# A two-stage encoder trunk on one core: its engine queues put in order by the context's timeline model instead of its default one

## The chip, the cores and the metric

The kernel runs on one core of one Trainium2 chip. A core has a matrix engine (TensorE, PE in the profile), a vector engine (DVE), a scalar engine (ACT), GpSimd (POOL) and a queue that issues transfers (SyncE, SP). Each engine works down one queue of instructions in the order in which the program lists them. The metric is the device time of one execution in microseconds (us), lower is better. Before the change the median of three runs was 2829.97 us, the lowest 2828.54 and the highest 2830.24.

## The reference, cut to what matters

A stream of 2048 frames with 1024 channels passes two layers.

- Layer 0: RMS norm, one projection to `u` and `z`; `u` goes through trailing means over 2, 4, 8 and 16 frames minus the frame itself, a linear map per channel group and a scale; times SiLU(z), an output projection, and a residual add. Then a gated embedding: `x + (p[0] @ ple_w[0]) * sigmoid(x @ ple_gate_w[0])`.
- From the stream after layer 0 one projection gives keys (RMS-normed) and values for 16 heads of 64 channels.
- Layer 1: RMS norm, a projection to `q` and `z`, RMS norm of `q` per head, strictly causal stick-breaking attention, times SiLU(z), output projection, residual add, and a second gated embedding.

The attention is what the second stage spends its time on:

```python
mask = s_idx < t_idx
log_keep = jnp.where(mask, jax.nn.log_sigmoid(-logits), 0.0)
later = lax.cumsum(log_keep, axis=log_keep.ndim - 1, reverse=True) - log_keep
log_a = jax.nn.log_sigmoid(logits) + later
a = jnp.where(mask, jnp.exp(log_a), 0.0)
```

So a weight is sigmoid(logit) times the product of (1 - sigmoid) over all later keys that are still visible. All inputs are float32, the output is float32 of 2048 x 1024.

## The kernel before, in words

Every float32 operand of a product is split into a high and a low part, and each product is three matmuls (high x high, high x low, low x high). The frames are cut into four chunks of 512.

**Stage one** runs layer 0, the key and value projection and the query projection, chunk by chunk, 22 steps for each chunk (`run_u`, `run_z`, `run_m`, `run_o`, `run_g`, `run_kvq`). A step is a product of 48 to 96 matmuls into a PSUM pool of six buffers (`psd`), and the vector, scalar and GpSimd engines empty it. Keys, queries, values and the split weights of stage two go to DRAM.

**Stage two** runs the attention. The loop goes over query chunks `c` = 3, 2, 1, 0, in each over 16 heads, and in each over the key chunks from the diagonal one backwards. One (query chunk, head, key chunk) is a slot of four sub-steps. Each sub-step has three parts, at three different sub-steps of the loop:

- `front`: two matmuls give 128 queries x 512 keys of logits (lines L602 and L603, tile `psl`, two buffers). ACT makes sigmoid(-logit) from it (L606, tile `kap`, four buffers). On the diagonal POOL masks a piece of it (L608). DVE scans it with a running product (L613, tile `pp`, 12 buffers).
- `turn`, six sub-steps later: PE transposes four 128 x 128 pieces of `pp` (L627) into a tile `psa`. ACT copies that to the high part of `at` (L630), DVE subtracts to get the low part (L631). `psa` has two buffers, so the transposes of a turn wait until L631 of the turn two earlier has read its buffer.
- `gather`, two sub-steps after the turn: PE multiplies the values with the high part (L639) and the low part (L640) into `pso`.

There are 160 slots and so 640 turns: 256 for c = 3, 192 for c = 2, 128 for c = 1, 64 for c = 0.

Beside the attention a generator of other matmuls, called fillers here (L668, L670, L672, 512 columns each), is pulled at a fixed rate: in c = 3 the gate projection `z` of the four chunks (`gate_z`), three matmuls per sub-step; in c = 2, 1 and 0 the output projection and the gated embedding of the chunk that was finished before (`post`). After the last slot `post(0)` runs alone.

```python
for n in range(4 * len(slots) + LAG_G):
    i2, j2 = divmod(n - LAG_T, 4)
    if 0 <= i2 < len(slots):
        turn(active[i2], j2)
    ...
        scan = front(active[i], j)
    if scan is not None:
        scan()
    owed += rate
    while owed >= 1.0:
        next(filler, None)
        owed -= 1.0
    ...
        gather(active[i3], j3)
```

**What sets the order.** The code above gives each instruction its place in a program, and that place is its priority. When the context closes, a scheduler plays the program through a model of the machine, and each time an engine is free it takes from the instructions that the model holds for ready the one with the earliest place. The order in which the model took them is then fixed as the engine's queue. A few instructions of stage one are tied to their place (`tc.keep_in_program_order`). On the chip nothing is rearranged any more: an instruction at the head of a queue that has to wait holds all those behind it.

## Time and profile before

| | |
|---|---|
| median of three runs | 2829.97 us (2828.54 to 2830.24) |
| profiled execution, first to last instruction (span) | 2822.5 us; no device time of its own is listed for it, 7.5 us less than the median |
| PE busy | 2747.1 us, 97% |
| DVE busy | 1892.6 us, 67% |
| ACT busy | 1409.9 us, 50% |
| POOL busy | 953.8 us, 34% |
| mean granted TensorE clock | 0.996 |

Stage one takes the first 1395 us of the span; the first turn of stage two starts at 1415.4 and the last at 2712.7 us; the rest is `post(0)`. PE is busy in nine tenths or more of all slices but two. DVE is half busy in stage one and nearly always busy in the first two thirds of stage two: 282.39 of the 300 us from 1600 on, 290.87 of the 300 us from 1900 on. A "busy" time of two neighbours on DVE overlaps a little, so the shares are a bit high.

### The profile page before, as it was taken

The numbers are of one execution on the slowest core, as the hardware profiler recorded it, in microseconds if no ns is written. First come the engines' busy times: TensorE is split into PE (matmuls) and PEld (weight loads), VectorE is DVE, ScalarE is ACT, GpSimd is POOL, SyncE is SP. The second block draws the span as 40 slices with busy tenths as digits, with TensorE's granted clock in tenths as the row PEclk, the third lists the DMA queues.
The fourth block names the chain that finished last, engine by engine and source line by source line (L and its number), as shares of the span: only waits on it lengthen the run. The fifth ranks groups of instructions, "written<-read, shape, count | busy, mean of one in ns | idle before, by whom it ended". The sixth has DMA issues, their size and how long they took to land. (4 is left out here: it accounts for less than half of the span.)

```text
span 2822.5 us, 40373 instructions
## 1 busy us (share of the span) xinstructions
PE 2747.1 (97%) x13667; PEld 2271.8 (80%) x13667; DVE 1892.6 (67%) x2581; ACT 1409.9 (50%) x2765; POOL 953.8 (34%) x965
## 2 busy tenths in 40 slices
PE   8999999999999999999899999999999999999999
PEld 6788788888888888888778888887878778878877
DVE  6655534555355543445289999999999998886642
ACT  5445523455244542445356555666666665664431
POOL 3564346643475425644211112121211122223220
PEclk9999999999999999999999999999999999999999
DMA  7855695557855678446666565455555565658765
GB/s 270 274 173 205 238 317 166 175 208 246 303 167 176 221 248 285 147 147 203 213 198 218 185 208 177 161 168 183 171 162 171 168 189 183 195 184 262 242 203 160
DMA packets 335139, 576.43 MB, mean 204 GB/s; under 512 B 32782, under 2 KB 161838, under 8 KB 334932
## 3 DMA queue, kind: packets, MB, share of 16 engines
q1 hardware_dynamic: 327944, 564.34, 60.8%
q10 hardware_dynamic: 6988, 9.50, 1.1%
q8 instruction: 108, 1.77, 0.3%
q14 instruction: 99, 0.81, 0.1%
HBM read 433.16 MB, written 132.19 MB: 200 GB/s over the span
## 5 line engine op out<-in xcount | busy, mean ns | idle before, releaser
L356 PE MATMUL psd<-wpair,x 128*128 128x512 f32 x2304 | 544.0, 393 | 0.0
L630 ACT CAST at<-psa 128x512 fp32r<-128x512 f32 (+3 forms) x640 | 333.4, 522 | 404.8 <-PE psa L627 399.9
L613 DVE TENSOR_TENSOR_SCAN pp<-kap,pp,zeros 128x512 f32<-128x512 f32 x384 | 511.7, 1334 | 5.0 <-ACT kap L606 2.8
L356 PEld LDWEIGHTS psd<-wpair,x 128*128 128x128 f32 x2304 | 428.1, 188 | 86.3
L631 DVE TENSOR_TENSOR at<-psa,at 128x512 fp32r<-128x512 f32 (+3 forms) x640 | 379.7, 595 | 59.2 <-ACT at L630 56.5
L627 PE MATMUL psa<-ident,pp 128*128 128x128 f32 x2176 | 347.4, 275 | 25.0 <-DVE at L631 20.4
L606 ACT ACTIVATE kap<-psl 128x512 f32<-128x512 f32 (+3 forms) x640 | 343.9, 538 | 17.0 <-PE psl L603 8.2
L627 PEld LDWEIGHTS psa<-ident,pp 128*128 128x128 f32 x2176 | 263.3, 140 | 102.8 <-DVE at L631 45.7
L608 POOL TENSOR_SCALAR_AFFINE_SELECT kap<-kap 128x128 f32<-128x128 f32 x256 | 91.7, 359 | 626.8 <-ACT kap L606 532.3
L602 PE MATMUL psl<-kk,qa 128*128 128x512 f32 (+3 forms) x640 | 281.3, 440 | 4.2 <-ACT vr L393 3.5
L613 DVE TENSOR_TENSOR_SCAN pp<-kap,zeros 128x128 f32<-128x128 f32 (+3 forms) x256 | 213.9, 836 | 40.5 <-POOL kap L608 37.0
L640 PE MATMUL pso<-at,vv 128*128 128x512 f32 (+3 forms) x640 | 235.4, 368 | 0.0
L603 PE MATMUL psl<-kk,qb 128*128 128x512 f32 (+3 forms) x640 | 234.6, 367 | 0.0
L639 PE MATMUL pso<-at,vv 128*128 128x512 f32 (+3 forms) x640 | 232.5, 363 | 1.3 <-ACT at L630 1.2
L127 PE MATMUL psd<-xp,wpair 128*128 128x512 f32 x512 | 200.2, 391 | 2.4 <-ACT xp L172 2.4
L111 DVE SCALAR_TENSOR_TENSOR wpair<-wraw,gains,wpair 128x512 fp32r<-128x512 f32 x192 | 149.6, 790 | 78.4 <-ACT wpair L110 78.1
L128 PE MATMUL psd<-xp,wpair 128*128 128x512 f32 x512 | 200.1, 391 | 0.0
L129 PE MATMUL psd<-xp,wpair 128*128 128x512 f32 x512 | 199.8, 390 | 0.0
L110 ACT ACTIVATE wpair<-wraw,gains 128x512 fp32r<-128x512 f32 x192 | 136.8, 720 | 113.2 <-DMA wraw<-in_w_kv_dram 69.2
L106 POOL TENSOR_TENSOR wpair<-wraw,wpair 128x512 fp32r<-128x512 f32 x107 | 146.0, 1369 | 62.1 <-ACT wpair L104 40.7
L104 ACT CAST wpair<-wraw 128x512 fp32r<-128x512 f32 x160 | 97.7, 619 | 114.2 <-PE psd L129 109.1
L639 PEld LDWEIGHTS pso<-at,vv 128*128 128x128 f32 x640 | 120.5, 188 | 28.4 <-ACT at L630 2.6
(204 smaller groups left out, 5488.9 us busy)
## 6 DMA issues: line engine op xcount, KB each, us to landing
wpair<-wi SPq DMA_DIRECT2D x96, 512.0 KB
kk<-kd SPq DMA_DIRECT2D x320, 128.0 KB
vv<-vd SPq DMA_DIRECT2D x160, 256.0 KB
wraw<-in_w_kv_dram SPq DMA_DIRECT2D x128, 256.0 KB
wpair<-wzd SPq DMA_DIRECT2D x64, 512.0 KB
wpair<-wod SPq DMA_DIRECT2D x64, 512.0 KB
wpair<-wgd SPq DMA_DIRECT2D x64, 512.0 KB
wi<-wpair SPq DMA_DIRECT2D x32, 512.0 KB
```

The lines of the kernel that those rows point to most:

```text
L127: T.matmul(ps, wst(units, kt, 0, c0), acts[kt][:, 0], start=(kt == order[0]), stop=False)
L128: T.matmul(ps, wst(units, kt, 0, c0), acts[kt][:, 1], start=False, stop=False)
L356: T.matmul(pss2[i], ck["x2"][kt][:, xh, tk], wst(ws, kt, wh, 0, W5), start=(kt == 0 and xh == 0 and wh == 0), stop=(kt == KT - 1 and wh == 1))
L602: T.matmul(ps[:, :w], qa[:, qs], kk[:, :w], start=True, stop=False)
L603: T.matmul(ps[:, :w], qb[:, qs], kk[:, :w], start=False, stop=True)
L606: A.activation(out=kp[:, r0:], in_=ps[:, :w], func=AF.Sigmoid, scale=-1.0)
L613: V.tensor_tensor_scan(out=pp[:, r0:][:, ::-1], data0=kp[:, r0:][:, ::-1], data1=zeros.to_broadcast([P, w]), initial=1.0 if st["diag"] els ...
L627: T.transpose(pt[:, j * P : (j + 1) * P], pp[:, r0 + kt * P : r0 + (kt + 1) * P], ident)
L630: A.copy(out=at[:, 0, cs], in_=pt[:, cs])
L631: V.tensor_tensor(out=at[:, 1, cs], in0=pt[:, cs], in1=f(at[:, 0, cs]), op=ALU.subtract)
L639: T.matmul(po[:, cs], vv[:, kt, :], at[:, 0, cs], start=(st["diag"] and kt == 0), stop=False)
L640: T.matmul(po[:, cs], vv[:, kt, :], at[:, 1, cs], start=False, stop=(st["last"] and kt == 3))
```

## The change

One argument of the context: the scheduler plays the program through the timeline model instead of the default one. The program, its priorities, its buffers and the number of arithmetic instructions stay the same.

```diff
-    with _tile.TileContext(nc) as tc:
+    with _tile.TileContext(nc, schedule_with_timeline_sim=True) as tc:
         trunk_kernel(tc, *args)
```

All five queues come out in another order. In stage one the matmuls of a product stay nearly where they were: no matmul of a product moves by more than about 9 us of PE work. In stage two the change is large. Instructions that only wait for a semaphore go from 411 to 572 on PE and from 719 to 1168 on DVE.

First place: PE, while the gate projection of an earlier chunk runs beside the attention of query chunk 3 (`xz` is that chunk's input, `psd` the fillers' result). Before:

```order
L627 MATMUL psa<-ident,pp 128x128 x4
L602 MATMUL psl<-kk,qa 128x512
L603 MATMUL psl<-kk,qb 128x512
L668 MATMUL psd<-xz,wpair 128x512
L670 MATMUL psd<-xz,wpair 128x512
L672 MATMUL psd<-xz,wpair 128x512
L639 MATMUL pso<-at,vv 128x512
L640 MATMUL pso<-at,vv 128x512
```

Each turn had its logits, three fillers and one gather. In the changed kernel the queue has this just ahead of the second such projection:

```order
L627 MATMUL psa<-ident,pp 128x128 x4
L640 MATMUL pso<-at,vv 128x512
L639 MATMUL pso<-at,vv 128x512
L627 MATMUL psa<-ident,pp 128x128 x4
L640 MATMUL pso<-at,vv 128x512
L639 MATMUL pso<-at,vv 128x512
L602 MATMUL psl<-kk,qa 128x512
L603 MATMUL psl<-kk,qb 128x512
```

and 15 rows further on:

```order
L627 MATMUL psa<-ident,pp 128x128 x4
L640 MATMUL pso<-at,vv 128x512
L627 MATMUL psa<-ident,pp 128x128 x4
L639 MATMUL pso<-at,vv 128x512
L668 MATMUL psd<-xz,wpair 128x512
L670 MATMUL psd<-xz,wpair 128x512
L672 MATMUL psd<-xz,wpair 128x512
L668 MATMUL psd<-xz,wpair 128x512
```

The fillers have left most turns and stand in bundles (14 in a row here). Counted over the queue, fillers in each group of eight turns of query chunk 3 (the first group takes in what stands ahead of the first turn):

```
before   42 21 24 24 24 24 24 24 24 24 24 24 24 24 24 24 24 24 24 24 24 24 24 24 24 24 24 24 24 24 24 9
changed 138 67 35 0 0 0 0 40 76 73 3 0 0 0 0 40 76 73 3 0 0 0 0 40 77 63 0 0 6 0 0 0
```

and of query chunk 2:

```
before  12 20 20 20 20 20 20 20 20 20 19 20 20 19 19 20 19 19 20 19 19 20 7 0
changed  2 65 78 29 0 0 0 0 0 0 85 41 0 30 19 11 30 19 13 4 0 2 4 0
```

Second place: DVE in query chunk 2, with buffer numbers (the `psa` number names the turn, the `kap` number one of its four buffers). Before:

```order
L631 TENSOR_TENSOR at_19021<-psa_19016,at_19021 128x512
L613 SCALAR_TENSOR_TENSOR pp_19036<-kap0_12853,zeros_12857 128x128
L631 TENSOR_TENSOR at_19047<-psa_19042,at_19047 128x512
L613 SCALAR_TENSOR_TENSOR pp_19057<-kap1_12854,zeros_12857 128x256
L631 TENSOR_TENSOR at_19069<-psa_19064,at_19069 128x512
L613 SCALAR_TENSOR_TENSOR pp_19079<-kap2_12855,zeros_12857 128x384
```

Now:

```order
L631 TENSOR_TENSOR at_19021<-psa_19016,at_19021 128x512
L613 SCALAR_TENSOR_TENSOR pp_19124<-kap0_12853,pp_19036,zeros_12857 128x512
L613 SCALAR_TENSOR_TENSOR pp_19142<-kap1_12854,pp_19057,zeros_12857 128x512
L613 SCALAR_TENSOR_TENSOR pp_19172<-kap2_12855,pp_19079,zeros_12857 128x512
L613 SCALAR_TENSOR_TENSOR pp_19189<-kap3_12856,pp_19100,zeros_12857 128x512
L631 TENSOR_TENSOR at_19047<-psa_19042,at_19047 128x512
L733 TENSOR_TENSOR xr_18955<-psd_18957,xr_18955 128x512
L733 TENSOR_TENSOR xr_19154<-psd_19156,xr_19154 128x512
L631 TENSOR_TENSOR at_19069<-psa_19064,at_19069 128x512
```

Scans and subtractions alternated; now four scans stand in a row ahead of one subtraction, and the scans belong to later slots than before. Counted over the 640 turns: exactly one scan stood ahead of a subtraction 610 times before and does 206 times now; no scan 18 and now 293 times; three or more 3 and now 95 times, of which 53 are runs of four.

## The prediction

> **What bounds the kernel now.** I read the page's span and busy times first, then the waits of PE, then the attention stage by stretches, then single turns in order of time.
>
> ```profile
> span 2822.5 us, 40373 instructions
> PE 2747.1 (97%) x13667; PEld 2271.8 (80%) x13667; DVE 1892.6 (67%) x2581; ACT 1409.9 (50%) x2765; POOL 953.8 (34%) x965
> PE psa L627 <- DVE at L631: 20.4, 40, 1.3
> PE psd L668 <- DMA wpair<-wzd: 6.4, 1, 6.4
> PE psao L765 <- DVE sg L760: 6.2, 4, 2.0
> ```
>
> PE stands still for 2822.5 - 2747.1 = 75.4 us in all. Every other order of the same matmuls can win at most that, 2.7%, and what it can lose has no such bound. The wait that recurs, 40 times, is the one of the transposes (L627) for DVE's subtraction (L631), which frees one of the two `psa` buffers; the longest of them is 1.3 us. The busy times by stretches, the columns being PE, PEld, DVE, ACT, POOL, granted clock, transfer share and GB/s:
>
> ```profile
> 0.00:100.00 100.00, 88.32 (x388) 71.61 (x389) 65.83 (x158) 50.45 (x114) 34.00 (x44) 1.00 0.79 276
> 100.00:1300.00 1200.00, 1188.16 (x5409) 982.50 (x5408) 594.58 (x839) 520.44 (x932) 605.33 (x518) 1.00 0.64 216
> 1415.00:1945.00 530.00, 518.74 (x2829) 429.02 (x2828) 499.15 (x597) 317.86 (x635) 101.34 (x111) 1.00 0.58 188
> 1945.00:2310.00 365.00, 353.90 (x1973) 291.96 (x1972) 349.06 (x444) 231.22 (x477) 66.79 (x93) 1.00 0.55 170
> 2310.00:2575.00 265.00, 256.38 (x1413) 213.73 (x1412) 226.22 (x304) 156.44 (x340) 63.05 (x97) 1.00 0.62 195
> ```
>
> Stage one has a PE that is full and a DVE, an ACT and a POOL that are half empty. The attention has two full engines: DVE is busy for 499 of 530 us and then for 349 of 365. There PE keeps its pace only because its work and DVE's are mixed evenly. Two neighbouring turns show how close the two are, first PE, then DVE (start, length, instruction):
>
> ```profile
> 1700.36 0.60 PE L627 MATMUL psa<-ident,pp 128*128 128x128 f32 x4
> 1700.71 0.47 PE L602 MATMUL psl<-kk,qa 128*128 128x512 f32 x1
> 1701.03 0.39 PE L603 MATMUL psl<-kk,qb 128*128 128x512 f32 x1
> 1701.25 0.39 PE L668 MATMUL psd<-xz,wpair 128*128 128x512 f32 x1
> 1701.48 0.40 PE L670 MATMUL psd<-xz,wpair 128*128 128x512 f32 x1
> 1701.72 0.39 PE L672 MATMUL psd<-xz,wpair 128*128 128x512 f32 x1
> 1701.95 0.40 PE L639 MATMUL pso<-at,vv 128*128 128x512 f32 x1
> 1702.18 0.39 PE L640 MATMUL pso<-at,vv 128*128 128x512 f32 x1
> 1702.41 0.60 PE L627 MATMUL psa<-ident,pp 128*128 128x128 f32 x4
> ```
>
> ```profile
> 2008.21 1.27 DVE L613 TENSOR_TENSOR_SCAN pp<-kap,pp,zeros 128x512 f32<-128x512 f32 x1
> 2009.41 0.66 DVE L631 TENSOR_TENSOR at<-psa,at 128x512 fp32r<-128x512 f32 x1
> 2009.99 1.27 DVE L613 TENSOR_TENSOR_SCAN pp<-kap,pp,zeros 128x512 f32<-128x512 f32 x1
> ```
>
> PE's turn is 1702.41 - 1700.36 = 2.05 us, of which the three fillers are 0.23 each. Without them it is 2.05 - 0.69 = 1.36 us. DVE's turn is 2009.99 - 2008.21 = 1.78 us: 1.20 for the scan and 0.58 for the subtraction, each started about 0.08 us before its neighbour's listed end. So a turn with fillers is PE's, and a turn without them is DVE's and costs PE 1.78 - 1.36 = **0.42 us of idle time**.
>
> **The change part by part.** No arithmetic instruction is added or removed, so the sum is made of idle time alone, against the profiled execution: 2822.5 us of span and 7.5 us around it (the median is 2829.97).
>
> *Fillers in bundles.* The counts per eight turns, shown with the change, say that in query chunk 3 the fillers stood at 24 in nearly every group and now stand at 40, 76, 73, 3, 0, 0, 0, 0. Groups with six fillers or fewer are 20 of 32 in chunk 3 and 13 of 24 in chunk 2: 160 and 104 turns that are now DVE's, 160 x 0.42 = 67 us and 104 x 0.42 = 44 us. In the bundles PE is the bound again and gives nothing back, since `psa` holds two turns and the `pp` tiles twelve. The same by a longer sum, which also takes in the narrow diagonal turns and what DVE does beside the turns: I added up, along each queue, the work between turns, cut it into windows of so many turns, and took of each window the larger of PE's, DVE's and ACT's sum. The row means are these (those of the narrower shapes likewise, DVE's less 0.075 for the overlap; PE 0.233 for 512 columns, 0.13 for a transpose, which makes PE's sum 1281 us):
>
> ```profile
> L613 DVE TENSOR_TENSOR_SCAN pp<-kap,pp,zeros 128x512 f32<-128x512 f32 x384 | 511.7, 1334 | 5.0 <-ACT kap L606 2.8
> L631 DVE TENSOR_TENSOR at<-psa,at 128x512 fp32r<-128x512 f32 x448 | 301.3, 674 | 37.4 <-ACT at L630 35.9
> L606 ACT ACTIVATE kap<-psl 128x512 f32<-128x512 f32 x448 | 269.6, 602 | 10.8 <-PE psl L603 6.7 <-DVE pp L613 0.5 <-issue 0.2
> L630 ACT CAST at<-psa 128x512 fp32r<-128x512 f32 x448 | 262.8, 587 | 331.4 <-PE psa L627 329.1 <-DVE pp L613 0.9 <-DVE at L631 0.9
> L627 PE MATMUL psa<-ident,pp x2176: 270/272/415, 1415.4 to 2712.7; 128*128 128x128 f32 x198
> ```
>
> The last row gives the truth of before: the turns take 2712.7 - 1415.4 = 1297 us.
>
> | window, turns | before | changed | changed less 1297 |
> |---|---|---|---|
> | 2 | 1341 | 1583 | 286 |
> | 3 | 1321 | 1494 | 197 |
> | 4 | 1308 | 1455 | 158 |
> | 8 | 1298 | 1410 | 113 |
> | 16 | 1290 | 1381 | 84 |
> | 32 | 1285 | 1344 | 47 |
>
> For the old order the window hardly matters, and eight turns give the measured time. For the new order the eight-turn window gives +113 us, by chunk 61, 34, 14 and 3 over the old order's own sums: that is the bundles' price, as the 67 and 44 say.
>
> *Scans in bursts.* What the shorter windows add comes from DVE's new order. Four scans in a row are 4 x 1.20 = 4.8 us in which no subtraction runs. PE may go on by two turns, 2 x 1.36 = 2.7 us without fillers, and then stands. There are 53 such runs and 41 of three. How much of it PE's own order lends out is not in the profile: below, the bound is the window of 32 turns (+47: the buffers lend all they can), above, the window of two (+286: `psa` lends two turns and nothing more). A burst of four scans with its subtraction spans about three turns of 1.78 us, so I take the middle of the windows of three and four: **+178 us**.
>
> *Gathers behind their own transposes.* Before, the high-part gather (L639) stood at the median 5.1 us of PE work behind the last transpose of its turn, now 1.7 us; in 42 turns less than 0.9 us, which is ACT's copy (0.587) and the semaphores on either side of it. The shortfalls add up to **+7 us**. In the others ACT hides it, as long as no sigmoid that waits for a scan's `kap` buffer stands ahead of the copy in ACT's queue; where one does, the copy is late, the gather behind it on PE, and then the next transposes. That is part of the upper bound.
>
> *Stage one.* The products keep their places within about 9 us of PE work, and `psd` has six buffers, three products of some 11 us each (48 matmuls of 0.23). DVE, ACT and POOL are at 595, 520 and 605 of 1200 us, so a late eviction is caught up before PE needs the buffer. I take 0, with -23 to +25: the idle time that stage one has now is 11.8 us in the second row of the stretches and 11.7 us in the first, and it may as well double. The load queue (SP) has its weight stores between the first frame loads now, which belongs to the same bound. The one-off wait of 6.4 us at the start of stage two stays, at 0 within 6.
>
> *Semaphores.* 449 more waiting instructions on DVE cost nothing by themselves; DVE's row shows them at 21 ns, under the instruction before:
>
> ```profile
> L631 DVEq EVENT_SEMAPHORE  x139: 21/21/21, 1439.8 to 2709.6; - x139
> ```
>
> Uncovered they would be 449 x 0.021 = 9 us.
>
> Sum: 2822.5 + 7.5 + 178 + 7 = **3015 us**, 6.5% slower.
>
> **The rivals.**
>
> *Faster: the new order fits the chip better.* An order made with truer lengths could remove the waits of the old one. For it speaks that the order was made by taking what was ready, so it can only place an instruction ahead of a late one, as with the `xz` matmuls. It wins at most the 75.4 us less the start; half of it gives 2830 - 37 = 2793 us. Against it: in chunk 3 DVE is 94% busy, and the filler-free groups need more DVE time than PE time whatever was assumed. It decides if the turns take less than 1297 us.
>
> *Slower, but little.* If scans that run ahead during a bundle lent PE the whole of the following stretch, the window of 32 would hold, +47, with stage one giving 20 back: 2857 us. Against it stands the `pp` pool: 12 buffers are 12 turns, the empty stretches are 32 to 48.
>
> *The clock falls too.* Where PE had waited long, the matmuls behind came 0.43 us apart instead of 0.23:
>
> ```profile
> 1404.32 0.77 PE L668 MATMUL psd<-x,wpair 128*128 128x512 f32 x1 [6.45 <-DMA wpair<-wzd]
> 1405.31 0.63 PE L672 MATMUL psd<-x,wpair 128*128 128x512 f32 x1
> 1405.74 0.63 PE L668 MATMUL psd<-x,wpair 128*128 128x512 f32 x1
> ```
>
> Nine matmuls at 0.2 us more are 1.8 us for such a stall. If each of the 53 four-scan bursts did it, 53 x 1.8 = 95 us more: 3110 us. A burst stalls PE for only 4.8 - 2.7 = 2.1 us by the count above, and waits of up to 1.3 us left the clock at 1.00 in these stretches. The Trainium skill ("TensorE: Matmul & The Clock Gate", "HAM oscillation — how this bites in real kernels") warns of PE-idle gaps over about 3.4 us; the 6.45 us gap agrees, and by that rule bursts of 2.1 us would keep the clock, so the sum would stay 3015.
>
> *The change does nothing.* The rows of the order exclude that the queues are the same; that the time is the same needs gains and losses to cancel.
>
> **How the numbers follow.** 0.2% is 5.7 us, about what a measurement of this kernel can tell from no change. The forecast (bundles and bursts, 2870 to 3120) has 0.81; slower than 3120, by the clock or by ACT's queue, 0.05; slower by little, 2836 to 2870, 0.04; the same 0.03; faster 0.07. The range is 2870 (the window of 16 with stage one and the start giving back: 2830 + 84 - 29 = 2885, a little below it) to 3120 (the window of two: 2830 + 286). Slower in all: 0.81 + 0.05 + 0.04 = 0.90.
>
> **What would show it.** In the changed profile the turns should take about 1480 us instead of 1297; PE's waits for L631 should grow from 20 us to over 100 and become the largest; PE in 40 slices should fall in the second half of the span, periodically in chunk 3, while DVE stays full there; stage one should end within 15 us of 1395; the clock in stage two should stay over 0.95. I am wrong on the bundles if PE stays at nine tenths in chunk 3, and on the bursts if the idle time in chunk 2 sits in other waits than those for L631 or `pp`.

## The result, and the profile after

| | before | changed | ratio, 95% interval |
|---|---|---|---|
| median (four runs each) | 2829.26 us | 3053.62 us (3051.07 to 3056.34) | 1.0792 [1.0777, 1.0807] |
| span of the profiled execution | 2822.5 us | 3053.1 us | |
| PE busy / idle in the span | 2747.1 / 75.4 us | 2829.3 / 223.8 us | |
| first to last turn of stage two | 1415.4 to 2712.7: 1297.3 us | 1406.7 to 2947.4: 1540.7 us | |

The change makes the kernel 224 us slower. The turns take 243 us more, the way to the first turn 9 us less. The page of the changed kernel, its totals:

```profile
span 3053.1 us, 41201 instructions
PE 2829.3 (93%) x13667; PEld 2285.5 (75%) x13667; DVE 1919.9 (63%) x2581; ACT 1431.3 (47%) x2765; POOL 986.9 (32%) x965
```

The engines have the same arithmetic instructions as before (PE 13667, DVE 2581, ACT 2765, POOL 965). Even so PE's busy time grows by 82 us, and that of the other three by 21 to 33 us. Stage one and the four query chunks by stretches (columns as before: PE, PEld, DVE, ACT, POOL, clock, transfer share, GB/s):

```profile
100.00:1300.00 1200.00, 1198.13 (x5467) 992.75 (x5466) 622.23 (x840) 524.72 (x937) 602.67 (x519) 1.00 0.64 214
1406.70:2036.00 629.30, 544.24 (x2768) 425.66 (x2769) 485.65 (x579) 318.82 (x614) 106.45 (x110) 0.98 0.50 152
2036.00:2483.00 447.00, 379.33 (x1929) 288.83 (x1928) 341.44 (x434) 234.06 (x468) 70.28 (x89) 0.97 0.45 134
2483.00:2780.00 297.00, 264.81 (x1408) 213.36 (x1406) 226.55 (x306) 159.42 (x339) 75.77 (x95) 0.98 0.58 175
2780.00:2950.00 170.00, 164.86 (x871) 139.28 (x872) 106.96 (x167) 82.43 (x194) 53.34 (x73) 0.99 0.76 227
```

Stage one lost 10 of its 11.8 us of idle time. In chunk 3 PE is busy for 544 of 629 us and DVE for 486: both stand about. A mean over bundles and filler-free turns says little of either, so I split the chunk into its groups of eight turns by the fillers that start in them. In the 96 turns of the groups with more than six fillers PE is 98% busy. In the 160 turns of the other groups, called filler-free below, which take 319.5 us, DVE is busy for 278.4 us (87%) and PE for 75%. That is the first thing to read here: without fillers not one engine became the bound, they wait for each other. The waits say how. Before, DVE's wait at the subtraction was

```profile
DVE at L631 <- ACT at L630: 56.5, 123, 1.9
```

Now the engines wait so:

```profile
PE psa L627 <- DVE at L631: 141.8, 164, 1.8
PE psl L602 <- ACT kap L606: 29.6, 65, 0.9
DVE at L631 <- ACT at L630: 168.6, 156, 4.1
DVE pp L613 <- PE psa L627: 122.9, 93, 6.2
ACT kap L606 <- DVE pp L613: 106.9, 208, 1.6
```

PE waits for DVE's subtraction, DVE's subtraction for ACT's copy, DVE's scan for PE's transposes (all twelve `pp` buffers are taken), ACT's sigmoid for DVE's scan (all four `kap` buffers are). Sixteen microseconds of chunk 3, DVE first:

```profile
1678.77 4.81 DVE L613 TENSOR_TENSOR_SCAN pp<-kap,pp,zeros 128x512 f32<-128x512 f32 x4
1683.49 1.26 DVE L631 TENSOR_TENSOR at<-psa,at 128x512 fp32r<-128x512 f32 x2
1685.64 0.69 DVE L631 TENSOR_TENSOR at<-psa,at 128x512 fp32r<-128x512 f32 x1 [0.89 <-ACT at L630]
1686.90 1.28 DVE L613 TENSOR_TENSOR_SCAN pp<-kap,pp,zeros 128x512 f32<-128x512 f32 x1 [0.57 <-PE psa L627]
1688.10 0.67 DVE L631 TENSOR_TENSOR at<-psa,at 128x512 fp32r<-128x512 f32 x1
1688.69 3.62 DVE L613 TENSOR_TENSOR_SCAN pp<-kap,pp,zeros 128x512 f32<-128x512 f32 x3
```

and PE at the same time:

```profile
1680.73 0.51 PE L602 MATMUL psl<-kk,qa 128*128 128x512 f32 x1 [0.50 <-ACT kap L606]
...
1684.30 0.63 PE L627 MATMUL psa<-ident,pp 128*128 128x128 f32 x4 [0.43 <-DVE at L631]
...
1688.91 0.63 PE L627 MATMUL psa<-ident,pp 128*128 128x128 f32 x4 [1.26 <-DVE at L631]
...
1693.04 0.52 PE L627 MATMUL psa<-ident,pp 128*128 128x128 f32 x3 [1.53 <-DVE at L631]
1693.31 0.48 PE L640 MATMUL pso<-at,vv 128*128 128x512 f32 x1
1694.72 0.69 PE L627 MATMUL psa<-ident,pp 128*128 128x128 f32 x2 [0.93 <-DVE at L631]
```

After four scans (4.81 us) DVE makes two subtractions, the two that `psa` had lent, and then has nothing: the third turn's transposes could only start at 1684.30, when the first subtraction had freed a buffer, the copy follows them, and DVE has lost 0.89 us. One more scan, which itself waited 0.57 us for PE, and PE stands for 1.26 us; three more, and it stands for 1.53 us. So a burst costs twice, PE during it and DVE behind it. During the four scans PE also stood three times (0.50, 0.45 and 0.50 us, the first is shown) ahead of logits: they waited for ACT's sigmoids, and those for the `kap` buffers that the scans had not read yet.

### The profile page after: what moved, and what is told of

It is laid out like the page before. It is cut to its first block, busy times and chain, and to the rows that moved or that the text cites. A ratio compares the mean times of both kernels' runs of the same rounds, so it can differ in the third digit from the quotient of the medians.

```text
span 3053.1 us, 41201 instructions
## 1 busy us (share of the span) xinstructions
PE 2829.3 (93%) x13667; PEld 2285.5 (75%) x13667; DVE 1919.9 (63%) x2581; ACT 1431.3 (47%) x2765; POOL 986.9 (32%) x965
## 4 chain that ended last, share of the span: by engine, by line
PE 73%; DVE 16%; DMA 4%; issue 4%; ACT 2%; POOL 1%; ACTq 0%; SPq 0%; DVEq 0%; POOLq 0%
PE psd L356 16%; DVE pp L613 10%; PE psd L128 7%; PE psd L127 7%; PE psd L129 7%; PE psa L627 6%; PE psd L668 5%; PE psd L670 5%; PE psd L672 5%; DVE at L631 4%; PE psl L602 2%; PE pso L640 2%; PE pso L639 2%; PE psl L603 2%; DMA vs<-vr 1%
## 5 line engine op out<-in xcount | busy, mean ns | idle before, releaser
L613 DVE TENSOR_TENSOR_SCAN pp<-kap,pp,zeros 128x512 f32<-128x512 f32 x384 | 490.5, 1313 | 80.2 <-PE psa L627 75.0
L630 ACT CAST at<-psa 128x512 fp32r<-128x512 f32 (+3 forms) x640 | 331.6, 522 | 394.0 <-PE psa L627 359.3
L627 PE MATMUL psa<-ident,pp 128*128 128x128 f32 x2176 | 358.7, 282 | 143.3 <-DVE at L631 141.8
L631 DVE TENSOR_TENSOR at<-psa,at 128x512 fp32r<-128x512 f32 (+3 forms) x640 | 372.9, 597 | 170.3 <-ACT at L630 168.6
L627 PEld LDWEIGHTS psa<-ident,pp 128*128 128x128 f32 x2176 | 262.3, 143 | 261.6 <-issue 105.2
L606 ACT ACTIVATE kap<-psl 128x512 f32<-128x512 f32 (+3 forms) x640 | 336.5, 534 | 218.2 <-DVE pp L613 106.9
L608 POOL TENSOR_SCALAR_AFFINE_SELECT kap<-kap 128x128 f32<-128x128 f32 x256 | 144.0, 569 | 764.5 <-ACT kap L606 753.8
L640 PE MATMUL pso<-at,vv 128*128 128x512 f32 (+3 forms) x640 | 288.0, 450 | 0.0
L602 PE MATMUL psl<-kk,qa 128*128 128x512 f32 (+3 forms) x640 | 252.8, 398 | 35.8 <-ACT kap L606 29.6
L613 DVE TENSOR_TENSOR_SCAN pp<-kap,zeros 128x128 f32<-128x128 f32 (+3 forms) x256 | 206.3, 836 | 65.6 <-PE psa L627 47.9
L639 PE MATMUL pso<-at,vv 128*128 128x512 f32 (+3 forms) x640 | 242.8, 379 | 0.5 <-ACT at L630 0.2
L111 DVE SCALAR_TENSOR_TENSOR wpair<-wraw,gains,wpair 128x512 fp32r<-128x512 f32 x192 | 165.1, 875 | 96.5 <-ACT wpair L110 96.1
L602 PEld LDWEIGHTS psl<-kk,qa 128*128 128x128 f32 x640 | 127.6, 199 | 89.2 <-ACT kap L606 69.7
```

The source lines that it names most:

```text
L602: T.matmul(ps[:, :w], qa[:, qs], kk[:, :w], start=True, stop=False)
L606: A.activation(out=kp[:, r0:], in_=ps[:, :w], func=AF.Sigmoid, scale=-1.0)
L613: V.tensor_tensor_scan(out=pp[:, r0:][:, ::-1], data0=kp[:, r0:][:, ::-1], data1=zeros.to_broadcast([P, w]), initial=1.0 if st["diag"] els ...
L627: T.transpose(pt[:, j * P : (j + 1) * P], pp[:, r0 + kt * P : r0 + (kt + 1) * P], ident)
L630: A.copy(out=at[:, 0, cs], in_=pt[:, cs])
L631: V.tensor_tensor(out=at[:, 1, cs], in0=pt[:, cs], in1=f(at[:, 0, cs]), op=ALU.subtract)
```

## The experiments

All pins named here tie an instruction behind the one that precedes it in the program on its engine (`tc.keep_in_program_order`); the scheduler then plays the program anew, so that the other queues can come out differently too.

**PE's stage two in program order, the rest free.** Every matmul and transpose of stage two is pinned, such as

```diff
-            T.matmul(ps[:, :w], qa[:, qs], kk[:, :w], start=True, stop=False)
+            tc.keep_in_program_order(T.matmul(ps[:, :w], qa[:, qs], kk[:, :w], start=True, stop=False))
```

> The changed kernel, but all matmuls and transposes of stage two stay in program order on PE (the other engines are free). Theory (the loss of 224 us is stage two's order on PE and what follows from it on DVE; the scheduler's stage one is harmless): about 2820 us, that is 2829 less the 9 us by which the first turn came earlier in the changed profile (1406.8 instead of 1415.4). Rival (part of the loss is DVE's and ACT's own order, whatever PE does): above 2870.

Measured: 2816.08 us (2813.36 to 2818.48), ratio to before 0.9958 [0.9944, 0.9972]. With PE in program order the whole loss is gone, and the timeline model's stage one is a gain: PE's idle time between 100 and 1300 us fell from 11.8 to 1.9 us. With PE fixed the model leaves ACT's sigmoids and copies alternating in 634 of 640 turns by itself, and DVE's scans and subtractions in 592. So this run does not part PE's order from the other two: with PE in order they come out in order as well. This kernel is faster than both; against the kernel before it gains 12 us.

```profile
0.00:100.00 100.00, 89.81 (x383) 71.09 (x384) 73.69 (x165) 54.59 (x122) 40.00 (x48) 0.98 0.90 324
100.00:1300.00 1200.00, 1198.15 (x5470) 992.32 (x5469) 620.53 (x841) 525.15 (x935) 601.53 (x518) 1.00 0.64 214
1415.00:1945.00 530.00, 526.14 (x2891) 438.84 (x2890) 502.97 (x604) 318.98 (x638) 77.33 (x110) 1.00 0.59 187
```

**Only the fillers pinned.**

```diff
-                T.matmul(ps, wst(units, kt, 0, c0), acts[kt][:, 0], start=(kt == 0), stop=False)
+                tc.keep_in_program_order(T.matmul(ps, wst(units, kt, 0, c0), acts[kt][:, 0], start=(kt == 0), stop=False))
```

and so the other two of `piecewise`.

> The changed kernel, but the fillers may not go ahead of the matmul that precedes them in the program: in query chunk 3 they are back near 24 for each eight turns, while DVE still has scans in bursts (51 runs of three, 49 of four) and the gathers stand close behind their transposes (median 2.1 us). Theory of the prediction (bundles 113, bursts about 65 and more): the bundles' part goes, 3054 - 113 = 2940, with what bursts cost left, some 110 over before. Rival A, bundles do all of it: under 2860. Rival B, bursts and close gathers do all of it: over 3020.

Measured: 3048.79 us. Undoing the bundles gives back 5 us. Rival B had the number; the prediction's share for the bundles in this kernel is refuted.

**Only scans and subtractions pinned.**

```diff
-            V.tensor_tensor(out=at[:, 1, cs], in0=pt[:, cs], in1=f(at[:, 0, cs]), op=ALU.subtract)
+            tc.keep_in_program_order(V.tensor_tensor(out=at[:, 1, cs], in0=pt[:, cs], in1=f(at[:, 0, cs]), op=ALU.subtract))
```

and so `V.tensor_tensor_scan`.

> The changed kernel, but scans and subtractions stay in program order on DVE: one scan ahead of each subtraction in 634 of 640 turns, the fillers still in bundles (36, 57, 58, 41, 0, 0, 0, 0 in each eight turns of chunk 3). Theory of the prediction: the bursts' part goes, 3054 - 65 = 2990 or less, the bundles' 113 stay, so not under 2930. Rival A, bundles do all: 3050. Rival B, bursts do all: 2850.

Measured: 2956.70 us, 97 us less. The bursts are worth more than the 65 us given to them, and 128 us stay. With DVE in order the filler-free turns are DVE's, as the prediction had it: in 136 of them in chunk 3 DVE is busy for 229.3 of 232.0 us. So what stays is, in chunk 3 at least, the bundles' cost.

**Bundles alone, in the default order.**

```diff
-            owed += rate
+            owed += rate * (64 / 24 if (n - n0) % 64 < 24 else 0) if n < 4 * 144 else rate
```

(`n0` is the sub-step at which the query chunk began.)

> The kernel before with its default order, but the loop pulls the fillers of chunks 3, 2 and 1 in bundles: 64/24 of the rate in the first 24 of each 64 turns and none in the other 40. Scans and subtractions go on alternating (571 of 640 turns). Theory: DVE's turn sets the pace of the turns without fillers, 0.42 us of idle time in each: about 160 + 104 + 56 turns, 0.42 x 320 = 134 us at most, 113 by the eight-turn sum, so 2830 + 113 = 2943 us. Rival B (bundles are lent out by the buffers and cost little without bursts): under 2870.

Measured: 2952.88 us, 125 us over before. The price worked out for the bundles was right where nothing else is wrong, and so was the mechanism: in the 136 filler-free turns of chunk 3 DVE is busy for 229.9 of 230.6 us. PE waits for L631 in 236 small pieces:

```profile
PE psa L627 <- DVE at L631: 103.4, 236, 1.6
```

So bundles cost 125 us alone and 5 us on top of the other parts. The parts do not add up. My reading is that where PE and DVE already hold each other up, the turns without fillers lose little further.

**Bursts alone, in the default order.** The scans of a slot are held until its last sub-step, and scans and subtractions are pinned as above:

```diff
-            if scan is not None:
-                scan()
+            held += [scan] if scan is not None else []
+            while j == 3 and held: held.pop(0)()
```

> The kernel before with its default scheduler and its even fillers, but the loop holds back the four scans of a slot until its last sub-step, and scans and subtractions are tied to that order on DVE: 160 runs of four scans, then four subtractions. Theory (psa lends two turns, then the chain transposes, ACT copy, subtraction runs alone): from the subtraction that ends ahead of a burst, 4.8 us of scans, two subtractions 1.2 us, then two turns that go one after another, PE's turn of 2.05 and twice copy and subtraction with their semaphores, some 9.2 us for a slot of which PE needs 8.2: about 1 us x 160 slots, 2990 us, and up to 3050 where a chunk has fewer fillers. Rival (the cost in the changed order comes from the gathers that stand close behind their transposes, not from the runs of scans): under 2860.

Measured: 3026.60 us, 198 us over before, 1.24 us for each of 160 bursts, a quarter more than the count.

**Runs of two.** `while j % 2 and held` in place of `j == 3`.

> The same, but two scans at a time: 317 runs of two. Theory: two scans are 2.4 us, less than the two turns that psa lends (2.7 us without fillers, 4.1 with three each), so PE never stands for it: under 2850 us. Rival (every departure from alternating costs in proportion to its length): about half of what the runs of four cost.

Measured: 2881.41 us, 52 us over before: 0.17 us for each of 317 runs. Not nothing, as the theory said, and not half of the runs of four (99 us), as the rival said. With runs of two 2.4 us long the loan of two turns nearly holds. What it does not cover are mostly places where DVE has something else to do as well: of the 63 waits of L627 for L631 that are left (60.6 us), 44 (42.9 us) have an instruction other than a scan or a subtraction among DVE's last five, which holds of only 277 of 638 subtractions.

**Is it `psa` or `kap`?** A run of four also leaves the sigmoids behind it without a buffer. The same kernel with eight of them:

```diff
-        NK = 4
+        NK = 8
-        wpair = st.enter_context(tc.tile_pool(name="wpair2", bufs=6))
+        wpair = st.enter_context(tc.tile_pool(name="wpair2", bufs=4))
```

> The default kernel with runs of four scans (3027 us with four kap buffers), but eight kap buffers, so that no sigmoid waits for a scan (to make room, four filler weight buffers instead of six). Theory (a run of four costs because psa lends only two turns): it stays, 2990 to 3030. Rival (a run of four costs because the sigmoids behind it find no kap buffer and hold the copies behind them on ACT): under 2900.

Measured: 3035.64 us, 6 us over the theory's range and far from the rival's. The cost stays with `kap` buffers to spare. PE's idle time in the turns grew by 160 us over before, and its waits for the buffers of `psa` by 155 us (175.4 less 20.4): in the default order it is the loan of `psa`.

```profile
PE psa L627 <- DVE at L631: 175.4, 111, 3.0
DVE at L631 <- ACT at L630: 300.3, 285, 3.1
```

**Fillers and DVE pinned together.**

> The changed kernel with both parts undone, fillers not ahead of their place on PE and scans and subtractions in program order on DVE. What is left of the changed order are the gathers: median 2.4 us behind their transposes instead of 5.1, and the low-part gather behind the next turn's transposes. Theory (bundles and runs of scans are the whole loss): 2815 to 2835 us. Rival (the close gathers and the altered neighbours on PE, L640 at 450 ns instead of 368, cost by themselves): above 2870.

Measured: 2948.86 us. The theory fell: with even fillers and alternating scans 120 us of the loss are still there. The rival had the number, but the waits of this kernel point to another cause than its gathers:

```profile
PE psl L602 <- ACT kap L606: 66.3, 88, 10.6
PE psa L627 <- DVE at L631: 42.1, 80, 1.8
ACT kap L606 <- DVE pp L613: 389.9, 440, 2.3
DVE at L631 <- ACT at L630: 224.3, 186, 5.0
```

ACT waits at a sigmoid for a scan, 440 times, and DVE at a subtraction for ACT's copy. The timelines of ACT and DVE show the knot:

```profile
1691.17 0.60 ACT L606 ACTIVATE kap<-psl 128x512 f32<-128x512 f32 x1 [1.18 <-DVE pp L613]
1691.69 0.63 ACT L711 ACTIVATE sgz<-zr 128x512 f32<-128x512 f32 x1
1692.23 1.06 ACT L630 CAST at<-psa 128x512 fp32r<-128x512 f32 x2
```

```profile
1689.80 1.28 DVE L613 TENSOR_TENSOR_SCAN pp<-kap,pp,zeros 128x512 f32<-128x512 f32 x1
1690.99 0.66 DVE L709 TENSOR_TENSOR zr<-psd,rb 128x512 f32<-128x512 f32 x1
1692.83 0.69 DVE L631 TENSOR_TENSOR at<-psa,at 128x512 fp32r<-128x512 f32 x1 [1.17 <-ACT at L630]
```

The sigmoid at ACT's head needs the `kap` buffer of the scan that ends at 1691.1. The copy of a turn whose transposes ended at 1690.6 stands behind it and behind a sigmoid of the fillers (L711), and DVE's subtraction stands for 1.17 us behind the copy. Counted over the queues: sigmoids that stand ahead of a turn's copy on ACT although their scans stand behind that turn's subtraction on DVE, in number of turns:

```
                      0     1     2     3     4 ahead
before              629     9     2     0     0
changed             206    95   100    93   146
DVE pinned            9    14   162   310   145
fillers, DVE pinned  15    19    65   393   148   (one of the 15 is behind)
```

Four ahead is all that four `kap` buffers allow: then scan, sigmoid, copy and subtraction run one after another. Note the third row: it is the pin on DVE that tightens this knot, since it moves scans back behind subtractions while the sigmoids stay early on ACT. Three or four stand ahead in 239 turns of the changed kernel, in 455 with DVE pinned and in 541 here.

**ACT pinned as well.** Also

```diff
-            A.copy(out=at[:, 0, cs], in_=pt[:, cs])
+            tc.keep_in_program_order(A.copy(out=at[:, 0, cs], in_=pt[:, cs]))
```

and so the sigmoid.

> The changed kernel with fillers kept behind their predecessors on PE, scans and subtractions in program order on DVE, and now sigmoids and copies in program order on ACT. The gathers still stand close behind their transposes (median 2.2 us). In the kernel with only the first two (2949 us) a sigmoid that waits for a kap buffer stands ahead of the copy: counted over the queues, three or four not yet scanned sigmoids ahead of the copy in 541 of 640 turns, now none in 634. Theory (ACT's head of queue is the third part of the loss): 2815 to 2835 us. Rival (the close gathers cost by themselves): still 2930 to 2950.

Measured: 2879.27 us (2877.63 to 2883.76), 70 us less than without it, ratio to before 1.0186 [1.0169, 1.0203]: between the theory and the rival. So ACT's queue is worth 70 us in that kernel, where the pins had tightened the knot; what it is worth in the changed kernel this does not show. 51 us are left. PE's largest wait is now

```profile
PE pso L639 <- ACT at L630: 43.2, 28, 3.6
```

The longest 25 of the 28 (42.4 us) all come about in the same way, and it is ACT's queue once more. The first of them:

```profile
1479.88 0.42 PE L640 MATMUL pso<-at,vv 128*128 128x384 f32 x1
1481.79 0.39 PE L639 MATMUL pso<-at,vv 128*128 128x256 f32 x1 [1.49 <-ACT at L630]
```

```profile
1480.21 1.28 ACT L651 ACTIVATE os<-os,en 128x128 f32<-128x128 f32 x4 [1.31 <-DVE os L645]
1481.39 0.35 ACT L630 CAST at<-psa 128x256 fp32r<-128x256 f32 x1
```

```profile
1478.17 1.27 DVE L613 TENSOR_TENSOR_SCAN pp<-kap,pp,zeros 128x512 f32<-128x512 f32 x1
1479.48 0.69 DVE L645 TENSOR_TENSOR os<-pso,os 64x512 f32<-64x512 f32 x1
```

At the end of each pair of heads four activations (L651, not pinned) stand ahead of a turn's copy on ACT. In all but one of the 25 they wait for an addition on DVE (L645), here one that stands behind a scan, and the copy and the gather wait with them. A gather that stands 5.1 us behind its transposes can bear that, one at 2.2 us cannot. The changed kernel has the close gathers too, but there PE's idle time ahead of L639 is 0.5 us in all, and L651 waits 12.5 us for L645 against 49.3 here: this part of the 51 us comes with the pins. The clock adds an estimated 17 us: in the turns of this kernel it was halved for 46 us (before: 3 us).

**More `kap` buffers instead of another order.** The kernel with fillers and DVE pinned, `NK = 8` and four weight buffers as above.

> The changed kernel with fillers and DVE in order (2949 us with four kap buffers), but eight kap buffers and four filler weight buffers. The scheduler then lets the sigmoids run further ahead: seven or eight not yet scanned ones ahead of the copy in 489 of 640 turns, of eight buffers, where it was three or four of four. Theory (a copy is held whenever the sigmoid ahead of it needs the buffer of a scan that is just ahead of the copy's own subtraction, whatever the number of buffers): still over 2900. Rival (more buffers take the wait away): 2815 to 2850.

Measured: 2952.73 us, the same as with four (2948.86). The scheduler filled the new buffers with further sigmoids (seven ahead in 389 turns), as the theory had it.

**Only ACT pinned.**

> The changed kernel with nothing but sigmoids and copies in program order on ACT. DVE's order then comes out alternating (586 of 640 turns), the fillers stay in bundles (36, 61, 66, 29, 0, 0, 0, 0). Theory (bundles cost some 120 wherever the rest is in order, bursts and ACT's queue the remainder): 2829 + 125 - 9 = 2945. Rival A (ACT's queue is all of it): 2820. Rival B (it is none of it): 3050.

Measured: 2981.12 us, 73 us less than the changed kernel, 36 us over the theory and far from both rivals. DVE alternates, ACT alternates, and 153 us are left. In the 144 filler-free turns of chunk 3 DVE is busy for 239.7 of 248.7 us, so most of it is the bundles (125 alone); the gathers' waits for late copies are there too (L639 for L630: 46.2 us in 18 pieces), and the clock is halved for 96 us of the turns. It is 24 us slower than with DVE alone pinned (2956.70), although there three or four sigmoids stand ahead of the copy in 455 turns and here none or one: beside bundles, putting ACT in order gained nothing, though the late copies that this pin brings may hide a gain.

**PE and DVE pinned**, ACT free.

> The changed kernel with PE's stage two in program order, and DVE's scans and subtractions too. Theory: DVE then waits nowhere out of turn; at or a few us under the 2816 us of the kernel with PE alone in program order (its idle time in the turns is 30 us). Rival (DVE's freedom is what lets it put evictions of fillers early): 5 to 20 us slower than that.

Measured: 2822.72 us, ratio 0.9976 [0.9967, 0.9985]; with PE alone pinned it was 0.9958 [0.9944, 0.9972]. The theory, at or under 2816, missed. The two intervals overlap slightly, so the rival's 5 to 20 us (6.6 measured) is likely, not shown.

## Why the prediction came out right, and where its steps did not

The time, 3053.6 us, lies in the range, and the direction and the size (224 us lost, 185 forecast) hold. The place is right as well: the loss is in stage two's order, and with PE's stage two back in program order the time is 2816 us. The steps:

- *"the sum is made of idle time alone".* This did not hold. In the turns PE's idle time grew by 156 us (34.1 to 190.0), its busy time by 87 us (1263.5 to 1350.9). By my estimate two things make most of the 87. A matmul that nothing follows at once is listed with about 0.39 us, one in a row starts 0.23 us ahead of the next, so each stall hides some 0.17 us in a busy row: 305 stalls at full clock instead of 74 give 39 us. And the halved clock gives 27 us. The first is idle time under another name; the second had been put at nothing.
- *PE at its limit, nothing to win.* Right in stage two. What could be won was in stage one, 10 us, inside the bound of -23 to 25, and the changed kernel won it.
- *Fillers in bundles, +113 us.* The price of the mechanism was right (125 us alone); its place in the sum was wrong. Taking the bundles out of the changed kernel gave 5 us. The step that failed is "a turn without them is DVE's": in the changed kernel DVE is not full in those turns (278.4 of 319.5 us in chunk 3, where bundles alone had 229.9 of 230.6), since it waits itself, and a turn takes 2.00 us instead of the 1.78 of the sum (1.70 with bundles alone). The prediction said that DVE would stay full in chunk 3; it did not.
- *Scans in bursts, what the shorter windows add.* The mechanism is shown in the default order (198 us for 160 runs of four, 52 us for 317 runs of two, and no less with eight `kap` buffers). The size was too small: undoing the runs gave 97 us where 65 had been given, and that with ACT's knot tightened by the same pin. The windows took the largest of three sums of work and left out that behind a burst DVE waits for a chain (transposes, copy), as the rows of 1683 to 1686 us show.
- *Gathers close behind, +7 us, with ACT's queue in the upper bound only.* The gathers by themselves were nearly right: in the changed kernel PE's idle time ahead of them is 0.5 us. The sentence that a sigmoid ahead of the copy makes the copy late, and with it the next transposes, described what happens; I had not counted how often it stands there (239 of 640 turns with three or four ahead), and had no term for it in the sum. What it is worth in the changed kernel is open: 70 us with fillers and DVE pinned, where it stands so in 541 turns, and no gain beside the bundles.
- *Semaphores, nothing.* No run tells the cost of 449 more waiting instructions on DVE by itself.
- *The clock stays.* Not quite. It did stay over 0.95, as forecast: the stretches of the turns ran at a mean of 0.98, 0.97, 0.98 and 0.99, before 1.00 in the first three. But in the trace's clock records it fell to 0.50 in 17 pieces of the turns, 68 us in all (before: one piece of 3 us), which by the estimate above cost 27 us. It had a rival of its own, 95 us and so 3110 us; it came in part. That rival's price lay inside the range of the forecast, so the time could not have told the two apart.

So 113 + 65 + 7 gave a total near the truth (185 of 224 us) out of parts that were not the right ones, inside a range of 250 us: that the number came so close is in part luck. The terms for bundles and bursts were each real alone, but in the mixture they hide behind each other, and waits on each other that the windows left out came on top. Undone one after another the steps are: DVE's runs 97, bundles 8 more, ACT's queue 70 more, the rest of PE's order 56 more (to 2823 us with PE and DVE pinned). Another order of undoing gives other steps, and a pin can bring in a loss of its own, as the runs with ACT pinned show; only the total is a property of the kernel.

What is still open: how much of the 224 us is ACT's queue. No run has ACT in order and everything else as the changed kernel has it; with ACT pinned alone, DVE's scans come out alternating too.

## What to carry to other kernels

In this kernel two engines are both over nine tenths busy and the buffers between them hold two pieces of work, and there the order in the queues alone was worth 224 us. In such a place compare how evenly each queue mixes its kinds of work, and for each wait at a queue's head ask what stands behind it on that engine. A window sum came near the size of the loss here, but not its parts; undo the parts one by one and together, since they hide behind each other, and count the other queues again after each pin, since they move too. And a scheduler's model can be let loose on the part of a program with slack (here stage one, 10 us of idle time) while the tight part is pinned: 2816 us beats both orders.

## What the runs showed of the hardware that was not expected

The clock of TensorE fell without any long gap. In the sixteen microseconds shown above PE's gaps were 1.26, 1.53 and 0.93 us, with eight and two short groups of work between them. In the trace's clock records the clock is 0.50 from 1694.15 us, inside the third gap, to 1700.98 us (the columns are those of the stretches):

```profile
1695.00:1701.00 6.00, 6.00 (x23) 5.49 (x23) 4.96 (x8) 2.48 (x7) 3.31 (x3) 0.50 0.30 89
1701.00:1706.00 5.00, 4.52 (x29) 3.55 (x28) 3.58 (x7) 3.28 (x7) 0.29 (x1) 1.00 0.30 88
```

In the first of them PE was busy all the time and did 23 instructions in 6 us, in the second 29 in 4.52 us. Two matmuls of 512 columns from the first are 0.42 us apart, against 0.23 us at full clock:

```profile
1698.20 0.63 PE L602 MATMUL psl<-kk,qa 128*128 128x512 f32 x1
1698.62 0.63 PE L603 MATMUL psl<-kk,qb 128*128 128x512 f32 x1
```

So a stall is paid for once more behind it. The longest gap of PE in all turns of the changed kernel was 1.85 us, and the clock still fell 17 times, each time for 3.41 or 6.83 us. What goes with a fall here is the sum of the gaps: in the 3.41 us ahead of each PE had stood for 1.28 to 2.38 us. That sum does not part the cases cleanly in this kernel, since stretches with up to 1.81 us of gaps kept the clock. With runs of four scans in the default order it comes out sharper: of all stretches of 3.41 us at full clock, counted in step with the falls, the 16 in which PE stood longest, 1.90 to 2.82 us, are those ahead of the 16 falls.

The prediction kept the clock by a rule of the Trainium skill ("TensorE: Matmul & The Clock Gate", "HAM oscillation — how this bites in real kernels"), which warns of PE-idle gaps over about 3.4 us; by these traces that rule is too lenient. The Trainium skill has on the same page, in "A second HAM failure mode: psum-queue depth-cycling", that PE's short idle times between groups of matmuls can make the clock swing. This trace agrees, with gaps of 0.93 to 1.53 us.

A matmul that follows a group of transposes takes longer in the records, whichever it is: with 512 columns 477 ns in the median and 0.31 us to the next start, others 394 ns and 0.23 us. Before, that was mostly the logits' first matmul (L602, mean of all widths 440 ns), and the low-part gather had 368; in the changed order, where L640 mostly follows the transposes, it has 450 and L602 398:

```profile
L640 PE MATMUL pso<-at,vv 128*128 128x512 f32 (+3 forms) x640 | 288.0, 450 | 0.0
L602 PE MATMUL psl<-kk,qa 128*128 128x512 f32 (+3 forms) x640 | 252.8, 398 | 35.8 <-ACT kap L606 29.6 <-DMA kk<-kd 3.6 <-ACT vr L393 1.0
```

It hardly bears on PE's 82 us more of busy time: 449 matmuls of 512 columns followed transposes before, 469 do now.
